# The modulation vectors of a two-layer trunk: the sum over 128 partitions by block transposes and row sums on VectorE and one product, with the result per partition

## The chip, the cores and the metric

The kernel runs on one core of a Trainium2 chip. The metric is the device time of one execution in microseconds. Before the change it is 1592.36 us, the median of three runs (1592.27 to 1593.94). A measurement of this kernel tells a difference of about 0.2% (3.2 us) from no change.

## The reference, cut to what matters

Two layers run over 256 latent tokens and 256 context tokens of width 1024. In each layer a conditioning vector `c` and a learned context vector `c_ctx` are turned into six modulation vectors of 1024 each; they scale and shift the tokens ahead of the mixer and ahead of the MLP, and gate what the two sub-layers add.

```python
def ada_mod(cond, w, b):
    return jnp.split(jax.nn.silu(cond) @ w + b, 6, axis=-1)
...
        sh1, sc1, g1, sh2, sc2, g2 = ada_mod(c[:, None, :], w_ada[l], b_ada[l])
        csh1, csc1, cg1, csh2, csc2, cg2 = ada_mod(c_ctx, w_ada[l], b_ada[l])
...
        u = x * (1.0 + sc1) + sh1
        p = split_proj(u @ w_in[l] + b_in[l])
...
        x = layer_norm(DEEPNORM_ALPHA * x + g1 * y, ln_g[l, 0], ln_b[l, 0])
        x = layer_norm(DEEPNORM_ALPHA * x + g2 * sq_relu_ffn(x * (1.0 + sc2) + sh2, w_ff1[l], w_ff2[l]),
                       ln_g[l, 1], ln_b[l, 1])
```

`w_ada[l]` is 1024 x 6144 in float32. The rest of a layer is a projection to 76 tiles of 128 channels, four branches (two convolutions, differential attention, neighbourhood attention), a merge by gates, an output projection and a squared-ReLU MLP of 4096.

## The kernel before

The large products are made on TensorE out of two parts of each float32 operand, a rounded one and what is left over: ScalarE writes the rounded part of a weight (`whi`), VectorE the rest (`wlo`), and three products are summed. The weights come in units of 128 x 1024 elements (512 KB) in one fixed order; each is loaded into a tile `raw`, split into `whi` and `wlo`, and used by 24 products or so. The tiles `raw`, `whi`, `wlo` and `araw` share ten buffers, at most three of each of the first three and two `araw` (`CAPS_W`). The step of this weight order that TensorE has reached is called the pace.

The order of all instructions on every engine is fixed ahead of the run by a planner. Each part of the work is a generator that yields one operation after another, with a priority (a smaller number goes first). The planner keeps a clock for each engine, gives each operation an assumed cost and puts next the operation that can start first, the one with the smaller number among equals. The engines then run their lists in that order, each instruction waiting for its own inputs. Where the planner sees TensorE without work for more than 0.8 us, it puts transposes of the identity in front (L272), whose results nobody reads. All loads and stores are issued by SP, in one list.

Priorities near the change: weight splits 3, merge of the branches 11, attention 10 to 16, the modulation of layer 0 12 and of layer 1 27 (`PRIO_ADA`), the long convolution's taps 90.

The modulation stands in `ada`. Group (0, 0), layer 0's first 2048 columns, has its own path at the start (`ada_first`) and isn't touched. The other five groups (l, g) of 2048 columns, (0, 1), (0, 2), (1, 0), (1, 1) and (1, 2), run one after another, (0, 1) from pace 44 (`ADA_PACE0`) and layer 1's from pace 108 in steps of 16. A group loads w_ada in 16 pieces `araw`, and VectorE, with ScalarE for some of the first ones, multiplies each row by the silu of the condition and sums over the eight blocks of 128 rows, into eight tiles `sums` of 128 x 512: four column blocks q by two conditions. Four of these tiles are borrowed from the four buffers `pad`, which the convolutions use too. What then is left is the sum over the 128 partitions:

- TensorE multiplies each `sums` with a matrix `ones` of 32 columns, one of which is 1: eight products with 512 columns, four column blocks side by side in the array, into `ada`.
- VectorE adds the bias (`ba`, loaded with b_ada repeated over 32 partitions) and writes `adrow`: the result along the free dimension, on a few partitions.
- TensorE transposes `adrow` in four blocks (`adT`), and VectorE copies 32 columns of it into `modT`: the result per partition, as the scaling of u needs it.
- For the gates (g > 0) four DMAs write rows of 2 KB from `adrow` to DRAM (`g`), from where they are later spread over the partitions as `row`.

The path that reads `modT` is `affine` and `to_u`; the path that reads `g` is `row_bcast`.

Of the kernel before, what the change touches and what calls it, by code (L numbers as in the profile page):

```python
# [9 lines left out]
F32 = mybir.dt.float32  # L10
# [25 lines left out]
ADA_PACE0 = 44  # L36
ADA_STEP = 16
ADA_SUMS = {(0, 1), (0, 2), (1, 0), (1, 1), (1, 2)}
# [283 lines left out]
class Kernel(Sched):  # L322
# [209 lines left out]
    def constants(self):  # L532
# [16 lines left out]
        self.ones = self.const([128, 2, 32], "ones")  # L549
        nc.vector.memset(self.ones.ap, 0.0)  # L550
        for c in range(2):
            nc.vector.memset(self.ones.ap[:, c, c:c + 1], 1.0)
# [11 lines left out]
        self.x2 = V(self.dp.tile([256, 1024], F32, name="x2"), (Buf(None),))  # L564

# [180 lines left out]
    def ada(self, l, g, pace):  # L746

        nc = self.nc
        yield self.wait("cs")
        yield self.wait("pace", pace)  # L750
        ba = yield self.s("", F32, "ba")
        yield self.dma(ba, self.rows4(self.b_ada[l, g * 2048:(g + 1) * 2048].rearrange("(q n) -> q n", q=4)), 1 << 18)
        sums = None
        if (l, g) in ADA_SUMS:
            sums = []
            pads = []
            for q in range(4):
                x = yield self.alloc("pad", name="sums")
                y = yield self.s("sums", F32, "sums")
                pads.append(x)  # L760
                sums.append((x[:, 0:512], y))
        ps = None
        for k in range(KD):
# [7 lines left out]
            if sums:  # L771
                for q in range(4):
                    w = raws[q // 2][:, (q % 2) * 512:(q % 2) * 512 + 512]
                    for c in range(2):
                        x, y = sums[q][c], self.cs[:, k, c:c + 1]
                        yield self.stt(x, w, y, x, ALU.mult, ALU.add) if k else self.affine_any(x, w, y)
                self.release(*raws)
                continue
            if ps is None:
                ps = yield self.alloc("ps", "ada", name="ada")  # L780
            yield self.mm([(ps.ap[32 * q:32 * q + 32, :], self.cs.ap[:, k, :],
                            raws[q // 2].ap[:, (q % 2) * 512:(q % 2) * 512 + 512], k == 0, k == KD - 1,
                            {"tile_position": (0, 32 * q)}) for q in range(4)], [ps], [*raws, self.cs], 1017)
            self.release(*raws)
        if sums:
            ps = yield self.alloc("ps", "ada", name="ada")
# [24 lines left out]
        self.release(row)  # L811

    @staticmethod
    def rows4(b):

# [1138 lines left out]
```

## Time and profile before

| what | value |
|---|---|
| median of three runs | 1592.36 us (1592.27 to 1593.94) |
| the profiled execution, its time | 1594.69 us |
| the profiled execution, its span from first to last instruction | 1592.9 us |
| mean granted TensorE clock | 0.998 |
| TensorE's products and weight loads | 8815 each |
| VectorE | 1308.8 us busy, 82% of the span |
| ScalarE | 876.2 us busy, 55% of the span |
| moved by DMA | 254.32 MB, 160 GB/s in the mean |

The busy time of PE (TensorE's products) is that of modelled ends; where rows of the timeline follow one another on PE, the distance of two starts says what a product takes of the engine, and its duration is the longer time until its result stands. DVE is VectorE, ACT ScalarE, POOL GpSimd, SP the engine that issues DMAs. VectorE's instructions overlap by some 0.1 us too where the next doesn't need the last one's result.

### The profile page before, as it was taken

How to read it: one execution, taken by the hardware profiler on the slowest of the kernel's cores; microseconds unless marked ns; L12 is line 12 of the kernel's file. 1: busy time of each engine (PE TensorE's matmuls, PEld its weight loads, DVE VectorE, ACT ScalarE, POOL GpSimd, SP SyncE). 2: the span in 40 equal slices, each digit the busy share in tenths (PEclk: the TensorE clock that was granted, in tenths of full speed). 3: DMA queues.
4: the chain of work that ended last, by engine and by line, in shares of the span. 5: the costliest groups of instructions: out<-in, count | busy, mean ns of one | idle time of the engine just before them, and what ended most of it. 6: DMA issues, size and time to landing. Idle time of an engine off the chain costs nothing. (4 is left out here: it accounts for less than half of the span.)

```text
span 1592.9 us, 23283 instructions
## 1 busy us (share of the span) xinstructions
PE 1571.9 (99%) x8815; PEld 1347.7 (85%) x8815; DVE 1308.8 (82%) x2210; ACT 876.2 (55%) x1413; POOL 12.2 (1%) x51
## 2 busy tenths in 40 slices
PE   9999999999999999999999999999999999999997
PEld 7778888887888888887887878989997999999997
DVE  4899999799998648896886795999999796785566
ACT  3576376456655544742423324766576786466553
POOL 0000000000000000000000000000000000000000
PEclk9999999999999999999999999999999999999999
DMA  9422222545553245455565644533443445645563
GB/s 357 145 69 79 99 74 80 184 173 169 169 179 126 81 159 197 152 198 179 177 206 177 213 160 156 188 126 132 147 139 120 146 159 171 240 146 186 198 224 108
DMA packets 80997, 254.32 MB, mean 160 GB/s; under 512 B 9060, under 2 KB 13924, under 8 KB 80884
## 3 DMA queue, kind: packets, MB, share of 16 engines
q1 hardware_dynamic: 80884, 252.83, 46.8%
q8 instruction: 69, 1.13, 0.3%
q14 instruction: 44, 0.36, 0.1%
HBM read 250.66 MB, written 2.13 MB: 159 GB/s over the span
## 5 line engine op out<-in xcount | busy, mean ns | idle before, releaser
L442 PE MATMUL mm<-u,whi 128*128 128x512 f32 (+1 forms) x3248 | 803.2, 340 | 1.8 <-ACT u L388 1.1
L442 PEld LDWEIGHTS mm<-u,whi 128*128 128x128 f32 x3248 | 557.7, 190 | 71.9 <-ACT u L388 4.2
L388 ACT ACTIVATE whi<-raw 128x1024 fp32r<-128x1024 f32 (+1 forms) x342 | 359.6, 1052 | 336.6 <-DVE wlo L395 127.3
L442 PE MATMUL mm<-u,wlo 128*128 128x512 f32 (+1 forms) x1624 | 542.6, 339 | 1.2 <-DVE wlo L395 0.8
L395 DVE TENSOR_TENSOR wlo<-raw,whi 128x1024 fp32r<-128x1024 f32 (+1 forms) x342 | 415.8, 1217 | 139.6 <-PE mm L442 65.2
L442 PEld LDWEIGHTS mm<-u,wlo 128*128 128x128 f32 x1624 | 306.4, 190 | 36.0 <-DVE wlo L395 1.8
L442 PE MATMUL f<-whi,a 128*128 128x512 f32 (+1 forms) x760 | 236.3, 388 | 0.0
L422 DVE SCALAR_TENSOR_TENSOR sums<-araw,cs,sums 128x512 f32<-128x512 f32 x280 | 194.8, 748 | 9.6 <-DMA araw<-in_w_ada 9.4
L442 PEld LDWEIGHTS f<-whi,a 128*128 128x128 f32 x760 | 142.3, 188 | 31.2 <-issue 2.5
L442 PE MATMUL f<-wlo,a 128*128 128x512 f32 (+1 forms) x380 | 147.1, 387 | 0.0
L422 DVE SCALAR_TENSOR_TENSOR conf<-glu,sm,conf 128x512 f32<-128x512 f32 (+1 forms) x240 | 138.9, 618 | 1.0
L442 PEld LDWEIGHTS f<-wlo,a 128*128 128x128 f32 x380 | 71.4, 188 | 14.2
L388 ACT ACTIVATE P<-S,st 128x512 f32<-128x512 f32 (+1 forms) x96 | 58.5, 613 | 25.1 <-DVE st L1229 24.9
L442 PE MATMUL wo<-whi,mg 128*128 128x512 f32 (+1 forms) x184 | 56.5, 382 | 0.0
L1229 DVE TENSOR_REDUCE st<-S 128x1 f32<-128x512 f32 (+1 forms) x96 | 55.2, 594 | 0.2
L442 PE MATMUL S<-qk 128*128 128x512 f32 (+1 forms) x192 | 49.9, 370 | 4.1 <-ACT qk L388 1.5
L388 ACT ACTIVATE qk<-ra 64x512 fp32r<-64x512 f32 (+1 forms) x71 | 40.3, 567 | 23.6 <-DVE ra L395 21.1
L388 ACT ACTIVATE gth<-mm,hb 128x512 f32<-128x512 f32 (+1 forms) x64 | 36.8, 575 | 29.6 <-PE mm L442 29.4
L388 ACT ACTIVATE a2f<-mm 128x512 f32<-128x512 f32 (+1 forms) x64 | 30.7, 481 | 31.7 <-PE mm L442 31.7
L395 DVE TENSOR_TENSOR a<-a2f,a 128x512 fp32r<-128x512 f32 (+1 forms) x64 | 35.4, 557 | 11.0 <-ACT a L388 10.6
L388 ACT ACTIVATE bh<-br,hb 128x512 f32<-128x512 f32 (+1 forms) x64 | 36.2, 571 | 13.8 <-PE br L442 13.5
L442 PEld LDWEIGHTS S<-qk 128*128 128x128 f32 x192 | 31.9, 189 | 13.8 <-ACT qk L388 4.0
(216 smaller groups left out, 1878.3 us busy)
## 6 DMA issues: line engine op xcount, KB each, us to landing
raw<-in_W SPq DMA_DIRECT2D x338, 512.0 KB
araw<-in_w_ada SPq DMA_DIRECT2D x80, 512.0 KB
a<-in_w_ada SPq DMA_DIRECT2D x32, 256.0 KB
bt<-in_rpb SPq DMA_DIRECT2D x32, 128.0 KB
raw<-in_W SPq DMA_DIRECT2D x8, 384.0 KB
row<-g SPq DMA_DIRECT2D x12, 256.0 KB
x<-in_x_t SPq DMA_DIRECT2D x8, 256.0 KB
row<-in_ln_g SPq DMA_DIRECT2D x8, 256.0 KB
```

Source lines behind the costliest of these rows:

```text
L388: lambda: nc.scalar.activation(out=out.ap, in_=in_.ap, func=func, **kw),
L395: return self._op(eng, cost, lambda: e.tensor_tensor(out=out.ap, in0=x.ap, in1=y.ap, op=op), [out], [x, y])
L422: return self._op("DVE", cost, lambda: nc.vector.scalar_tensor_tensor(out=out.ap, in0=x.ap, scalar=a(s), in1=y.ap, op0=op0, op1=op1), [out ...
L442: nc.tensor.matmul(out=out, lhsT=x, rhs=y, start=start, stop=stop, **kw)
L1229: yield self.dve(68 + 1.04 * nk, lambda: nc.vector.tensor_reduce(out=mx.ap, in_=S.ap, axis=AX.X, op=ALU.max, negate=True), [mx], [S])
```

## The change

The sum over the partitions is made in another way. For each of the eight tiles `sums` of a group, VectorE transposes its blocks of 32 x 32 elements in place of the block (4 x 16 blocks of a 128 x 512 tile, into `sumT`), and then sums each run of 32 along the free dimension. After this, a partition holds a sum over 32 of the 128 partitions for 16 columns, and eight such results of 16 columns fill 128 columns of `red`, the first 128 columns of the first `sums` tile. One product with a constant 128 x 128 matrix `four`, which has a 1 where two partitions agree modulo 32, adds the four quarters and leaves the sums on all partitions. Four small VectorE additions pick the quarter that belongs to each 32 partitions, add the bias, and write `modT`. The transposes and row sums run at priority 20 (`PRIO_SUM`).

With it the row `adrow`, its four TensorE transposes and `ba` go. The bias comes with the layer's small constants (`bada`, 48 columns more in SM). The gates are written to DRAM from `modT`: two DMAs for a group, each from 128 partitions x 8 elements, to 1024 single elements of 4 bytes in the order of the channels. `ones` goes, `four` is made at the start out of the identity by one reduction and one copy on VectorE. `ADA_PACE0` is 40 where it was 44, and all groups take this path (as all five did before).

```diff
-ADA_PACE0 = 44
+ADA_PACE0 = 40
 ADA_STEP = 16
-ADA_SUMS = {(0, 1), (0, 2), (1, 0), (1, 1), (1, 2)}
+PRIO_SUM = 20
...
-               ("dng", 1), ("bbr", 32), ("lng", 16), ("lnb", 16)):
+               ("dng", 1), ("bbr", 32), ("lng", 16), ("lnb", 16), ("bada", 48)):
...
+    def same_of_32(self):
+        nc = self.nc
+        t = self.const([128, 32], "four1")
+        src = self.ident.ap.rearrange("p (a i) -> p i a", a=4)
+        yield self.dve(200, lambda: nc.vector.tensor_reduce(out=t.ap, in_=src, axis=AX.X, op=ALU.add), [t], [self.ident])
+        o, x = self.four.ap.rearrange("p (a i) -> p a i", a=4), t.ap.unsqueeze(1).to_broadcast([128, 4, 32])
+        yield self.dve(200, lambda: nc.vector.tensor_copy(o, x), [self.four], [t])
+        self.signal("four")
...
-        if sums:
-            ps = yield self.alloc("ps", "ada", name="ada")
-            for h in range(2):
-                yield self.mm([(ps.ap[32 * q:32 * q + 32, :], self.ones.ap[:, c, :], sums[q][c].ap, c == 0, c == 1,
-                                {"tile_position": (0, 32 * q)}) for c in range(2) for q in (2 * h, 2 * h + 1)], [ps],
-                              [*sums[2 * h], *sums[2 * h + 1], self.ones], 1000)
-            for x, y in zip(pads, sums):
-                self.release(x, y[1])
-        row = yield self.s("", F32, "adrow")
-        yield self.tt(row, ps, ba, ALU.add)
-        self.release(ps, ba)
-        t = yield self.alloc("ps", "att", name="adT")
-        yield self.transposes([t[:, b * 128:b * 128 + 128] for b in range(4)],
-                              [row[:, b * 128:b * 128 + 128] for b in range(4)])
...
+        yield ("prio", PRIO_SUM)
+        red = pads[0][:, 0:128]
+        for q in range(4):
+            for c in range(2):
+                x = sums[q][c]
+                yield self.dve(600, lambda: nc.vector.transpose(out=t.ap, in_=x.ap), [t], [x])
+                o, z = red[:, 64 * c + 16 * q:64 * c + 16 * q + 16], t.re("p (b j) -> p b j", j=32)
+                yield self.dve(600, lambda: nc.vector.tensor_reduce(out=o.ap, in_=z.ap, axis=AX.X, op=ALU.add), [o], [z])
         self.release(t)
+        yield ("prio", PRIO_ADA if l else 12)
+        self.release(*pads[1:], *[y for x, y in sums])
+        ps = yield self.alloc("ps", "ada", name="ada")
+        yield self.mm([(ps.ap[:, 0:128], self.four.ap, red.ap[:, 0:128], True, True, {})], [ps], [red, self.four], 220)
+        bias = self.sm[l][:, _SM["bada"] + 16 * g:_SM["bada"] + 16 * g + 16]
+        for a in range(4):
+            p = slice(32 * a, 32 * a + 32)
+            o = self.modT[l][p, 16 * g:16 * g + 16, :]
+            src = ps.ap[p, 0:128].rearrange("p (s k a) -> p k s a", s=2, a=4)[:, :, :, a]
+            b = bias.ap[p].unsqueeze(2).to_broadcast([32, 16, 2])
+            yield self.dve(95, lambda: nc.vector.tensor_tensor(out=o.ap, in0=src, in1=b, op=ALU.add), [o], [ps, bias])
...
+            k0 = 16 * g + (0 if g == 1 else 8)
             for s in range(2):
-                for j in range(2):
-                    q = j + (0 if g == 1 else 2)
-                    yield self.dma(self.grow[l][g - 1][s][:, j * 512:(j + 1) * 512],
-                                   row[32 * q + s:32 * q + s + 1, :], 2048)
+                yield self.dma(self.grow[l][g - 1][s].re("o (k r) -> r (o k)", r=128), self.modT[l][:, k0:k0 + 8, s], 1 << 18)
```

How the lists of the engines stand now, at three places. On PE before, group (0, 2) ends like this (`mm` are projections out of u, `PT`, `S` and `o` attention, `br` the branches' products):

```order
L442 MATMUL mm<-u,wlo 128x512
L442 MATMUL ada<-sums,ones 32x512 x8
L503 MATMUL PT<-ident,P 128x128 x8
L442 MATMUL S<-qk 128x512 x2
L503 MATMUL adT<-ident,adrow 128x128 x4
L442 MATMUL mm<-u,whi 128x512 x2
```

In the changed kernel PE's list has for the same group:

```order
L442 MATMUL mm<-u,whi 128x512 x2
L442 MATMUL mm<-u,wlo 128x512
L442 MATMUL ada<-sums,four 128x128
L442 MATMUL br<-yd,whi 128x512 x2
L442 MATMUL br<-yd,wlo 128x512
```

Eight products and four transposes have become one product, and it stands among the products of the last branch, `br<-yd`, where the eight stood among attention.

On DVE before, the end of group (0, 2), its last multiplications, `adrow` and the copy into `modT` (`mod_90`), lies among weight splits and attention (`yd`, `pt`):

```order
L422 SCALAR_TENSOR_TENSOR sums<-araw,cs,sums 128x512 x4
L395 TENSOR_TENSOR wlo<-raw,whi 128x1024
L395 TENSOR_TENSOR yd<-olo,yd 64x512
L395 TENSOR_TENSOR adrow<-ada,ba 128x512
L395 TENSOR_TENSOR pt<-PT,pt 128x512 x2
L801 COPY mod_90<-adT 128x32
```

In the changed kernel DVE's list has the transposes and row sums of this group nearly in one run:

```order
L788 STREAM_TRANSPOSE sumT<-sums 128x512
L395 TENSOR_TENSOR wlo<-raw,whi 128x1024
L790 TENSOR_REDUCE sums<-sumT 128x16
L788 STREAM_TRANSPOSE sumT<-sums 128x512
L790 TENSOR_REDUCE sums<-sumT 128x16
L788 STREAM_TRANSPOSE sumT<-sums 128x512
L790 TENSOR_REDUCE sums<-sumT 128x16
```

Sixteen instructions have come in where one addition and one copy stood, with a weight split between them here and there; they depend on one another pair by pair through the one tile `sumT`.

At the third place, on PE before, in the end of the neighbourhood attention of layer 0, the planner had put transposes of the identity in three gaps (`o<-ident`, `PT<-ident`):

```order
L442 MATMUL o<-pt,v 128x256 x8
L272 MATMUL o<-ident 128x128 x7
L442 MATMUL o<-pt,v 128x256 x4
L503 MATMUL PT<-ident,P 128x128 x4
L272 MATMUL PT<-ident 128x128 x5
L503 MATMUL PT<-ident,P 128x128 x4
L442 MATMUL o<-pt,v 128x256 x8
L272 MATMUL o<-ident 128x128 x6
L442 MATMUL o<-pt,v 128x256 x4
```

In the changed kernel this end of the attention is spread between projections, and PE's list there is:

```order
```order
L503 MATMUL PT<-ident,P 128x128 x8
L442 MATMUL mm<-u,whi 128x512 x2
L442 MATMUL mm<-u,wlo 128x512
L442 MATMUL mm<-u,whi 128x512 x2
L442 MATMUL mm<-u,wlo 128x512
L442 MATMUL o<-pt,v 128x256 x12
L503 MATMUL PT<-ident,P 128x128 x4
```

The eighteen transposes of the identity are gone, and six projections of u stand between the attention's transposes and the products that read them.

More of the change, by code (lines that the diff above doesn't have):

```diff
@@ L548, in constants @@
         nc.gpsimd.memset(self.cs.ap, 0.0)
[L549 to L552, printed above, removed]
+        self.four = self.const([128, 128], "four")
         self.free.update(DVE=900.0, POOL=900.0, SP=SP_START)
@@ L750, in ada @@
         yield self.wait("pace", pace)
[L751 to L762, printed above, removed]
+        t = yield self.s("", F32, "sumT")
+        sums = []
+        pads = []
+        for q in range(4):
+            x = yield self.alloc("pad", name="sums")
+            y = yield self.s("sums", F32, "sums")
+            pads.append(x)
+            sums.append((x[:, 0:512], y))
         for k in range(KD):
@@ L770, in ada @@
                 raws.append(raw)
-            if sums:
[L772 to L779, printed above, removed]
-                ps = yield self.alloc("ps", "ada", name="ada")
@@ L781, in ada @@
-            yield self.mm([(ps.ap[32 * q:32 * q + 32, :], self.cs.ap[:, k, :],
-                            raws[q // 2].ap[:, (q % 2) * 512:(q % 2) * 512 + 512], k == 0, k == KD - 1,
-                            {"tile_position": (0, 32 * q)}) for q in range(4)], [ps], [*raws, self.cs], 1017)
-            self.release(*raws)
-        if sums:
-            ps = yield self.alloc("ps", "ada", name="ada")
-            for h in range(2):
-                yield self.mm([(ps.ap[32 * q:32 * q + 32, :], self.ones.ap[:, c, :], sums[q][c].ap, c == 0, c == 1,
-                                {"tile_position": (0, 32 * q)}) for c in range(2) for q in (2 * h, 2 * h + 1)], [ps],
-                              [*sums[2 * h], *sums[2 * h + 1], self.ones], 1000)
-            for x, y in zip(pads, sums):
-                self.release(x, y[1])
@@ L793, in ada @@
-        row = yield self.s("", F32, "adrow")
-        yield self.tt(row, ps, ba, ALU.add)
-        self.release(ps, ba)
-        t = yield self.alloc("ps", "att", name="adT")
-        yield self.transposes([t[:, b * 128:b * 128 + 128] for b in range(4)],
-                              [row[:, b * 128:b * 128 + 128] for b in range(4)])
-        out = self.modT[l][:, g * 16:(g + 1) * 16, :].re("p (q b) s -> p q b s", q=4)
-        src = t.ap.rearrange("p (b q r) -> p q b r", b=4, q=4)[:, :, :, 0:2]
@@ L801, in ada @@
-        yield self.dve(110, lambda: nc.vector.tensor_copy(out.ap, src), [out], [t])
-        self.release(t)
+            for q in range(4):
+                w = raws[q // 2][:, (q % 2) * 512:(q % 2) * 512 + 512]
+                for c in range(2):
+                    x, y = sums[q][c], self.cs[:, k, c:c + 1]
+                    yield self.stt(x, w, y, x, ALU.mult, ALU.add) if k else self.affine_any(x, w, y)
+            self.release(*raws)
+        yield self.wait("four")
+        yield ("prio", PRIO_SUM)
@@ new lines, in ada @@
+        red = pads[0][:, 0:128]
+        for q in range(4):
+            for c in range(2):
+                x = sums[q][c]
+                yield self.dve(600, lambda: nc.vector.transpose(out=t.ap, in_=x.ap), [t], [x])
+                o, z = red[:, 64 * c + 16 * q:64 * c + 16 * q + 16], t.re("p (b j) -> p b j", j=32)
+                yield self.dve(600, lambda: nc.vector.tensor_reduce(out=o.ap, in_=z.ap, axis=AX.X, op=ALU.add), [o], [z])
+        self.release(t)
+        yield ("prio", PRIO_ADA if l else 12)
@@ L810, in ada @@
             self.signal("grow", l, g - 1)
-        self.release(row)
-    @staticmethod
-    def rows4(b):
-        return b.unsqueeze(1).to_broadcast([4, 32, b.shape[1]])
     def ada_first(self, j, raws):
@@ L1838, in build @@
             self.spawn(self.silu_c(), 0)
+            self.spawn(self.same_of_32(), 60)
             self.spawn(self.ada_all(), 12)
@@ L1895, in _layout @@
         put("lnb", f["ln_b"][l].reshape(16, 128).T)
+        put("bada", f["b_ada"][l].reshape(48, 128).T)
     cT = np.stack([f["c"].reshape(8, 128), f["c_ctx"].reshape(8, 128)], -1).transpose(1, 0, 2).reshape(128, 16)
```

3 lines of the change are left out of this document (2 added, 1 removed).

## The prediction

> **What bounds the kernel now.** First the page's busy times, then TensorE's waits, then the busy time by stage.
>
> ```profile
> span 1592.9 us, 23283 instructions
> PE 1571.9 (99%) x8815; PEld 1347.7 (85%) x8815; DVE 1308.8 (82%) x2210; ACT 876.2 (55%) x1413; POOL 12.2 (1%) x51
> ```
>
> PE is busy for all but 21.0 us of the span. So an instruction taken off PE's list is worth its whole place there, as long as what PE does next is ready that much earlier. The question is whether VectorE, which gets the work instead, can still feed PE. The busy time by stage (busy us of PE, PEld, DVE and ACT, with counts) says where it has room:
>
> ```profile
> 360.00:380.00 20.00, 20.00 (x90) 16.21 (x89) 20.00 (x35) 13.91 (x20) 0.00 (x0) 1.00 0.55 183
> 380.00:400.00 20.00, 20.00 (x110) 15.50 (x109) 20.00 (x35) 12.46 (x21) 0.00 (x0) 1.00 0.48 158
> 400.00:420.00 20.00, 20.00 (x97) 16.77 (x96) 19.20 (x33) 13.35 (x24) 0.00 (x0) 1.00 0.58 187
> 420.00:440.00 20.00, 20.00 (x96) 16.73 (x96) 19.72 (x31) 12.10 (x22) 0.00 (x0) 1.00 0.42 143
> ...
> 500.00:520.00 20.00, 20.00 (x119) 17.54 (x118) 16.30 (x34) 14.44 (x30) 0.00 (x0) 1.00 0.25 82
> 520.00:540.00 20.00, 19.57 (x118) 16.06 (x118) 15.83 (x32) 13.17 (x28) 0.00 (x0) 1.00 0.15 51
> 540.00:560.00 20.00, 20.00 (x90) 16.56 (x89) 8.88 (x10) 9.03 (x12) 0.00 (x0) 1.00 0.44 144
> 1000.00:1020.00 20.00, 20.00 (x111) 17.09 (x110) 18.13 (x33) 14.21 (x23) 0.55 (x1) 1.00 0.44 156
> 1020.00:1040.00 20.00, 20.00 (x171) 20.00 (x170) 19.72 (x36) 17.04 (x31) 1.84 (x10) 1.00 0.73 239
> ```
>
> From 360 to 440 us, where the first group ends, VectorE has 1.1 us of 80 left (0 + 0 + 0.80 + 0.28), and yet PE never stops: what fills VectorE there is in part work that nobody needs soon. From 500 to 560 it has 19.0 us left (3.7 + 4.17 + 11.12). In layer 1's attention both are short at once, and PE stops:
>
> ```profile
> 1040.00:1080.00 40.00, 38.51 (x199) 31.96 (x199) 39.46 (x90) 25.12 (x48) 0.00 (x0) 1.00 0.32 112
> 1120.00:1160.00 40.00, 38.76 (x263) 35.45 (x262) 39.39 (x85) 25.31 (x44) 0.13 (x2) 1.00 0.40 138
> 1200.00:1240.00 40.00, 38.34 (x206) 31.90 (x205) 37.70 (x79) 25.76 (x51) 0.00 (x0) 1.00 0.32 104
> ```
>
> 1.49 + 1.24 + 1.66 = 4.4 us of PE are lost in these three stretches.
>
> **What is taken off PE.** The products with `ones` by stage, one window for each group (the first and the last of five, and the sum), and then the timeline of PE around the first group's four transposes:
>
> ```profile
> 380.00:400.00 20.00, 2.47 (x16) 1.00 0.48 158
> ...
> 940.00:950.00 10.00, 1.94 (x16) 1.00 0.32 110
> sum 80.00, PE 12.52; mean PE 2.50
> ...
> 394.66 0.60 PE L503 MATMUL adT<-ident,adrow 128*128 128x128 f32 x4
> 395.02 0.71 PE L442 MATMUL mm<-u,whi 128*128 128x512 f32 x2
> ```
>
> 12.5 us for the products, in which almost nothing lies beside them, since PE's next product starts as they end. The four transposes hold PE from 394.66 to 395.02, 0.36 us; five groups make 1.8. Removed: 12.5 + 1.8 = 14.3 us.
>
> **What is put on PE.** One float32 product of 128 columns for each group. The nearest row is a constant float32 product of 256 columns:
>
> ```profile
> L442 PE MATMUL ms<-osq,on 128*128 128x256 f32 x8 | 2.4, 377 | 0.0
> ```
>
> That is 0.30 us for a record. The lists have 40 products with `ones` and the trace 80 records, so a float32 product makes two records, 0.60 us for 256 columns and 0.30 for 128. Bounds: 0.09 us, as one of the four transposes above (0.36 / 4), and 0.60, that row without the halving. I take 0.30, the row it is nearest to: 1.5 us for five.
>
> **Transposes of the identity.** The planner filled three gaps of the neighbourhood attention with them, and PE ran them:
>
> ```profile
> 529.19 0.93 PE L272 MATMUL o<-ident 128*128 128x128 f32 x7
> 529.87 1.08 PE L442 MATMUL o<-pt,v 128*128 128x256 f32 x4
> ...
> 531.22 0.71 PE L272 MATMUL PT<-ident 128*128 128x128 f32 x5
> 531.98 0.81 PE L503 MATMUL PT<-ident,P 128*128 128x128 f32 x4
> ...
> 533.90 0.81 PE L272 MATMUL o<-ident 128*128 128x128 f32 x6
> 534.47 0.74 PE L442 MATMUL o<-pt,v 128*128 128x256 f32 x2
> ```
>
> From their starts to the next product's: 0.68 + 0.76 + 0.57 = 2.0 us. In the new order projections of u stand in these gaps and the fillers are gone. So 2.0 us go if those projections were due anyway, and nothing if the wait turns up elsewhere. I count 2.0.
>
> **What VectorE gets.** Block transposes don't occur before. The nearest rows are the lane shuffle, which also moves elements between partitions, its neighbour of the same size, a row sum of 512, and the weight split of 1024 for a slower case:
>
> ```profile
> L1147 DVE STREAM_SHUFFLE rsh<-ra 128x256 f32<-128x256 f32 x16 | 7.1, 444 | 0.1
> L395 DVE TENSOR_TENSOR ra<-ra,rsh 128x256 f32<-128x256 f32 x16 | 6.7, 422 | 0.3
> L395 DVE TENSOR_TENSOR wlo<-raw,whi 128x1024 fp32r<-128x1024 f32 x334 | 408.1, 1223 | 139.1 <-PE mm L442 65.2 <-PE f L442 30.0 <-ACT whi L388 23.2
> L1229 DVE TENSOR_REDUCE st<-S 128x1 f32<-128x512 f32 x64 | 42.8, 683 | 0.1
> ...
> 981.03 0.69 DVE L395 TENSOR_TENSOR yf<-f,row 128x512 f32<-128x512 f32 x1 [0.30 <-PE f L442]
> 981.76 0.69 DVE L395 TENSOR_TENSOR yacc<-yf,yacc 128x512 f32<-128x512 f32 x1
> 982.37 1.22 DVE L395 TENSOR_TENSOR wlo<-raw,whi 128x1024 fp32r<-128x1024 f32 x1
> ```
>
> The shuffle takes as long as plain arithmetic (444 against 422 ns). So I take 0.69 us for a transpose of 512, as for arithmetic of 512. In the timeline an instruction that needs the one before starts 0.73 us after it (981.03 to 981.76), another 0.61 us (981.76 to 982.37). A pair of transpose and dependent row sum takes 0.73 + 0.61 = 1.34 us; eight pairs 10.7 us a group. The four additions at the end are worth about what `adrow` and its copy were:
>
> ```profile
> L395 DVE TENSOR_TENSOR adrow<-ada,ba x5: 672/691/699, 391.6 to 944.3; 128x512 f32<-128x512 f32 x5
> L801 DVE COPY mod<-adT x5: 182/187/198, 395.6 to 947.3; 128x32 f32<-128x32 f32 x5
> ```
>
> 0.69 + 0.19 = 0.88 us go, and four additions of 32 columns, at the copy's 0.19 each, cost 0.75. Net 10.7 us a group, 53 us in all. VectorE would be busy for about 1362 of 1580 us, 86%. Bounds for a transpose: 0.44 us (the shuffle's, were 512 as cheap as 256) and 1.22 us (the split of 1024, were each element to count twice).
>
> [...]
>
> **What hides these 53 us.** The new rows have priority 20. Weight splits (3), merge (11) and attention (10 to 16) go first, the convolution taps (90) and layer 1's multiplications (27) come later, so the group's own end and the next group are what is late. Counted by the products ahead of each in PE's list, at 0.227 us for 512 columns,
>
> ```profile
> 1433.54 21.79 PE f L442 x96
> ```
>
> (21.79 / 96), the five products stand 47, 54, 16, 35 and 79 us of products later than the first `ones` product of each group did. Layer 0's last group thus ends near 540 us, and its reader is `affine`; layer 1's last ends near 1015, and its reader is much later:
>
> ```profile
> L402 DVE TENSOR_SCALAR t<-mod x3: 168/168/169, 599.8 to 1373.1; 128x16 f32<-128x16 f32 x3
> ```
>
> 599.8 and 1373.1: nobody waits for `modT`. If the cover fails, a row that PE waits for comes behind a 0.7 us row of the new kind, up to 16 times a group. From 1000 to 1040 us, where the last group ends, VectorE has only 2.15 us left (1.87 + 0.28), so its taps move into the attention that already costs PE 4.4 us. I allow nearly half of that, 2.0 us, for new waits; bounds 0 and 21.4 (two groups, 10.7 each, in full stretches).
>
> **DMA and the rest.** The five loads `ba` and sixteen stores `g` go, eight stores of 1024 elements come, behind which SP's next weight loads queue. The loads' own row:
>
> ```profile
> q1 hardware_dynamic: 80884, 252.83, 46.8%
> ```
>
> 0.468 x 16 x 1592.9 us / 80884 = 147 ns for a packet of 3.1 KB in the mean. By bytes, 4 bytes cost nothing; at the mean packet's time, 64 packets on each of 16 engines take 9.4 us, 18.9 for a group's two stores. Packets of 4 bytes are nearer to nothing, and I count 0. The store itself is read only by `row`, long after it. The constants at the start grow by 128 x 48 x 4 bytes, 25 KB, a twentieth of one weight unit, and `four` is made while VectorE waits for the condition anyway:
>
> ```profile
> 2.62 0.17 DVE L402 TENSOR_SCALAR cth<-cth 128x16 f32<-128x16 f32 x1 [1.25 <-ACT cth L388]
> ```
>
> A start four weights earlier moves the first group's loads forward by 4 x 24 x 0.227 = 22 us, into a stretch without PE waits: 0.
>
> **The sum.** -14.3 + 1.5 - 2.0 + 2.0 = -12.8 us. The profiled span of 1592.9 becomes 1580.1; around it lie 1.8 us (its time is 1594.69), so that execution would take 1581.9. The runs' median is 2.3 us (0.15%) below that execution; from 1592.36 I get **1579.6 us**. With all waits absent and the bound of 0.09 us for the product it is 1592.36 - 14.3 + 0.5 - 2.0 = 1576.6.
>
> **Rivals.**
>
> - VectorE becomes the bound where it is full. For it: 1.1 us left from 360 to 440, 2.15 from 1000 to 1040. Against it: 19.0 us left from 500 to 560, and the low priority. If half the rows of the first and last group stand ahead of a row PE waits for, 10.7 us come back instead of the 0 from layer 0 and 2.0 from layer 1 counted: 1592.36 - 14.8 + 10.7 = 1588.3, between 1585 and 1592.
> - The stores of single elements hold up weight loads. Three loaded weights lie ahead of PE's use, each 24 x 0.227 = 5.4 us, 16.3 in all. At 18.9 us a group 2.6 us go through to PE, with the first transfer behind it some 3: four groups give 10 to 12 us, 1590 to 1592. Against it: a 4-byte packet at the price of a 3.1 KB one. [...]
> - Slower: a block transpose takes 1.22 us, not 0.69. The product `ada` stands in PE's list where the planner thinks 0.6 us for each, so PE waits at it: 0.54 x 8 = 4.3 us a group, 21.6 in five, 1579.6 + 21.6 = 1601. It turns the sign from 12.8 / 40 = 0.32 us more for each, above about 1.0 us. For it: no transpose in this trace; against it: the shuffle's row.
>
> **How the numbers follow.** The forecast gets 0.64, VectorE as the bound 0.16, the stores 0.07, the slow transpose 0.13. The bound of 0.2%, about what a measurement of this kernel can tell from no change, lies at 1589.2 and 1595.5. Of VectorE's 0.16, 0.09 fall under 1589.2, the rest on no change; the stores are no change; of the slow transpose 0.11 is slower and 0.02, with part of the wait hidden, no change. Faster 0.73, same 0.16, slower 0.11. The range reaches from 1576 (all waits absent) to 1595, which takes in the first two rivals with their bounds and leaves the slow transpose out.
>
> **What would show it.** In the changed profile: PE's records fall by 80 + 20 + 18 - 10 = 108; `ada<-sums,four` takes about 0.3 us a group; L788 and L790 take about 0.7 us each, some 53 us between them; nothing waits for `mod`; `wlo` rows still end ahead of their products. Wrong would be: waits of PE at `ada` of more than 1 us a group (slow transposes or full VectorE), waits of ScalarE's `whi` for DMA behind the stores (the second rival), or more than 2 us of new waits from 1040 to 1240.

## The result, and the profile after

| kernel | median | runs | ratio to before, 95% interval |
|---|---|---|---|
| before | 1592.45 us (1592.27 to 1593.94) | 4 | |
| changed | 1613.11 us (1612.14 to 1613.54) | 4 | 1.0129 [1.0117, 1.0141] |

The change makes the kernel 20.7 us slower; the forecast was 12.8 us faster. The changed kernel's profiled execution took 1612.14 us, with a span of 1610.3 and a mean granted clock of 0.991. Its busy times, from the page:

```profile
span 1610.3 us, 23122 instructions
PE 1563.9 (97%) x8707; PEld 1345.7 (84%) x8707; DVE 1360.9 (85%) x2304; ACT 874.1 (54%) x1408; POOL 11.9 (1%) x51
```

PE lost 108 records and VectorE got 52.1 us, both much as forecast. PE's busy time fell by only 8.0 us, where 14.8 were forecast; products at half clock, shown below, put some 7.3 us back. And PE is now idle for 46.4 us (1610.3 - 1563.9), where it was 21.0. The busy time by stage (columns as before: the stretch, its length, then PE, PEld, DVE, ACT and POOL, then granted clock) says where. The changed kernel:

```profile
440.00:480.00 40.00, 30.71 (x145) 25.48 (x144) 29.60 (x63) 20.96 (x42) 0.00 (x0) 0.87 0.51 122
520.00:560.00 40.00, 33.08 (x154) 27.15 (x153) 38.29 (x57) 14.53 (x21) 0.00 (x0) 0.91 0.39 131
880.00:920.00 40.00, 36.45 (x160) 29.55 (x159) 20.45 (x32) 13.02 (x18) 0.00 (x0) 1.00 0.68 180
1040.00:1080.00 40.00, 35.84 (x213) 30.40 (x212) 34.22 (x72) 21.92 (x39) 0.00 (x0) 0.95 0.56 164
```

The kernel before, in the same stretches:

```profile
440.00:480.00 40.00, 40.00 (x188) 33.41 (x188) 39.78 (x68) 23.55 (x41) 0.00 (x0) 1.00 0.56 191
520.00:560.00 40.00, 39.57 (x206) 32.62 (x206) 24.70 (x42) 22.20 (x39) 0.00 (x0) 1.00 0.30 97
880.00:920.00 40.00, 40.00 (x178) 33.10 (x178) 31.31 (x43) 12.34 (x16) 0.00 (x0) 1.00 0.68 220
1040.00:1080.00 40.00, 38.51 (x199) 31.96 (x199) 39.46 (x90) 25.12 (x48) 0.00 (x0) 1.00 0.32 112
```

Four holes of 9.3, 6.5, 3.6 and 2.7 us, 22.0 in all, and in three of them the granted clock falls too (0.87, 0.91 and 0.95). A busy PE at half clock counts as busy, so what this costs is not seen in the holes. Most of the rest of the new idle time lies between 960 and 1040 us. In the first, third and fourth hole VectorE, too, does less than before; in the second it does far more (38.29 against 24.70 us). They are two different things. PE's waits (engine and line, what it waited for, us in total, times, longest) name them:

```profile
PE PT L503 <- DVE P L402: 9.3, 1, 9.3
PE f L442 <- DVE wlo L395: 5.4, 4, 2.5
PE br L442 <- DVE yd L395: 3.5, 1, 3.5
PE S L442 <- DVE qk L402: 3.5, 5, 1.9
PE br L442 <- ACT yd L388: 3.1, 1, 3.1
```

**The first hole** is a DMA's. SP's own queue around it (start, us, what was issued):

```profile
441.40 1.01 SPq L433 DMA_DIRECT2D g<-mod  x2
442.50 0.53 SPq L433 DMA_DIRECT2D araw<-in_w_ada  x1
443.12 0.39 SPq L433 DMA_DIRECT2D raw<-in_W  x1
443.56 0.42 SPq L433 DMA_DIRECT2D bt<-in_rpb  x1
```

The two stores of group (0, 1)'s gates, 2048 single elements, are followed by three loads. The third is a small table, `bt`, of attention's biases. In VectorE's timeline its reader, and the four `sums` multiplications behind that, stand still:

```profile
449.78 0.16 DVE L1271 RECIPROCAL st<-st 128x1 f32<-128x1 f32 x1
458.42 0.43 DVE L395 TENSOR_TENSOR S<-S,bt 128x256 f32<-128x256 f32 x1 [8.48 <-DMA bt<-in_rpb]
458.76 1.67 DVE L402 TENSOR_SCALAR sums<-araw,cs 128x512 f32<-128x512 f32 x4
```

The load was issued at 443.56 and landed at 458.4, after 14.8 us, as `bt`'s own row says; its median is 3.6:

```profile
DMA to landing us min/median/max: 2.9/3.6/14.8
```

PE's wait of 9.3 us for `P` is this wait passed on: no row of `P` can be made until VectorE's list moves. The holes in the stretches from 880 and from 1040 us come behind layer 1's two pairs of stores; the last store is issued at 1036.3 us. Group (0, 2)'s pair, issued at 569 us, costs nothing: PE is busy for all of the 40 us from 560.

**The second hole** stands at the end of attention, where PE waits twice for `yd`. VectorE's timeline there:

```profile
541.77 2.73 DVE L422 SCALAR_TENSOR_TENSOR sums<-araw,cs,sums 128x512 f32<-128x512 f32 x4
544.53 0.69 DVE L395 TENSOR_TENSOR olo<-o,olo 64x512 f32<-64x512 f32 x1
545.25 2.74 DVE L422 SCALAR_TENSOR_TENSOR sums<-araw,cs,sums 128x512 f32<-128x512 f32 x4
547.91 1.22 DVE L395 TENSOR_TENSOR wlo<-raw,whi 128x1024 fp32r<-128x1024 f32 x1
549.16 0.69 DVE L395 TENSOR_TENSOR yd<-olo,yd 64x512 fp32r<-64x512 f32 x1
```

and PE's (in brackets the wait and what ended it):

```profile
545.93 0.50 PE L442 MATMUL br<-yd,whi 128*128 128x512 f32 x1 [3.15 <-ACT yd L388]
549.90 0.79 PE L442 MATMUL br<-yd,whi 128*128 128x512 f32 x1 [3.47 <-DVE yd L395]
```

What PE needs, `olo` and then `yd`, stands behind eight multiplications of group (0, 2), 5.5 us, whose result nobody needs for another 60 us.

**The clock** falls to a half in the first, second and fourth hole. Four narrow stretches of the changed kernel, first the first wait and what follows it, then what follows the second and the fourth hole:

```profile
456.90:466.40 9.50, 0.24 (x2) 0.00 (x0) 7.81 (x18) 5.28 (x9) 0.00 (x0) 0.73 0.50 167
466.40:471.40 5.00, 4.97 (x13) 4.01 (x14) 5.00 (x8) 2.40 (x5) 0.00 (x0) 0.50 0.38 113
549.90:553.30 3.40, 3.40 (x8) 2.72 (x9) 3.26 (x5) 1.63 (x2) 0.00 (x0) 0.50 0.23 93
1075.80:1082.60 6.80, 6.22 (x15) 4.88 (x16) 6.67 (x15) 3.67 (x8) 0.00 (x0) 0.51 0.01 2
```

After its wait of 9.3 us PE runs 5.0 us at clock 0.50. Products of 512 columns start 0.43 us apart there (469.69 to 470.12), and 0.23 us apart behind it (471.94 to 472.17), so about half of the stretch is lost, 2.5 us; the other two, counted in the same way, cost 1.7 and 3.1 us. These 7.3 us are counted as busy. While PE waits, a lower clock costs nothing: in the first stretch it is already down to 0.73. The length of the wait doesn't decide alone. The third hole, with 2.5 us as its longest wait, has a clock of 1.00; the fourth, with 1.9 us as its longest, has the most half clock.

### The profile page after: what moved, and what is told of

Read it like the earlier page. It is cut to its first block, busy times and chain, and to the rows that moved or that the text cites. A ratio compares the mean times of both kernels' runs of the same rounds, so it can differ in the third digit from the quotient of the medians.

```text
span 1610.3 us, 23122 instructions
## 1 busy us (share of the span) xinstructions
PE 1563.9 (97%) x8707; PEld 1345.7 (84%) x8707; DVE 1360.9 (85%) x2304; ACT 874.1 (54%) x1408; POOL 11.9 (1%) x51
## 5 line engine op out<-in xcount | busy, mean ns | idle before, releaser
L442 PE MATMUL mm<-u,whi 128*128 128x512 f32 (+1 forms) x3248 | 804.8, 341 | 2.3 <-ACT u L388 1.3
L442 PEld LDWEIGHTS mm<-u,whi 128*128 128x128 f32 x3248 | 557.3, 190 | 72.8 <-ACT u L388 4.6
L442 PE MATMUL mm<-u,wlo 128*128 128x512 f32 (+1 forms) x1624 | 542.5, 339 | 1.1 <-DVE wlo L395 1.1
L388 ACT ACTIVATE whi<-raw 128x1024 fp32r<-128x1024 f32 (+1 forms) x342 | 359.8, 1053 | 329.5 <-DVE wlo L395 99.9
L395 DVE TENSOR_TENSOR wlo<-raw,whi 128x1024 fp32r<-128x1024 f32 (+1 forms) x342 | 414.4, 1213 | 116.4 <-PE mm L442 44.0
L442 PEld LDWEIGHTS mm<-u,wlo 128*128 128x128 f32 x1624 | 306.1, 190 | 36.1 <-DVE wlo L395 1.9
L442 PE MATMUL f<-whi,a 128*128 128x512 f32 (+1 forms) x760 | 234.6, 387 | 0.0
L422 DVE SCALAR_TENSOR_TENSOR sums<-araw,cs,sums 128x512 f32<-128x512 f32 x280 | 196.0, 746 | 15.9 <-DMA araw<-in_w_ada 15.7
L442 PEld LDWEIGHTS f<-whi,a 128*128 128x128 f32 x760 | 142.3, 188 | 28.8
L442 PE MATMUL f<-wlo,a 128*128 128x512 f32 (+1 forms) x380 | 147.5, 388 | 5.4 <-DVE wlo L395 5.4
L422 DVE SCALAR_TENSOR_TENSOR conf<-glu,sm,conf 128x512 f32<-128x512 f32 (+1 forms) x240 | 137.6, 613 | 1.0
L442 PEld LDWEIGHTS f<-wlo,a 128*128 128x128 f32 x380 | 71.4, 188 | 21.3 <-DVE wlo L395 7.1
L388 ACT ACTIVATE P<-S,st 128x512 f32<-128x512 f32 (+1 forms) x96 | 58.7, 615 | 35.9 <-DVE st L1222 35.7
L442 PE MATMUL S<-qk 128*128 128x512 f32 (+1 forms) x192 | 50.0, 379 | 6.9 <-DVE qk L402 3.5
L442 PE MATMUL wo<-whi,mg 128*128 128x512 f32 (+1 forms) x184 | 56.5, 382 | 0.0
L388 ACT ACTIVATE qk<-ra 64x512 fp32r<-64x512 f32 (+1 forms) x67 | 37.8, 565 | 24.1 <-DVE ra L395 22.8
L388 ACT ACTIVATE gth<-mm,hb 128x512 f32<-128x512 f32 (+1 forms) x64 | 36.8, 575 | 21.4 <-PE mm L442 21.1
L442 PEld LDWEIGHTS S<-qk 128*128 128x128 f32 x192 | 33.1, 195 | 17.6 <-DVE qk L402 4.8
L388 ACT ACTIVATE bh<-br,hb 128x512 f32<-128x512 f32 (+1 forms) x64 | 36.3, 573 | 20.7 <-PE br L442 20.4
L503 PE MATMUL PT<-ident,P 128*128 128x128 f32 x240 | 36.1, 275 | 10.8 <-DVE P L402 9.3
L388 ACT ACTIVATE a2f<-mm 128x512 f32<-128x512 f32 (+1 forms) x64 | 30.7, 482 | 26.3 <-PE mm L442 26.3
```

Of the source, the lines that this page charges most:

```text
L388: lambda: nc.scalar.activation(out=out.ap, in_=in_.ap, func=func, **kw),
L395: return self._op(eng, cost, lambda: e.tensor_tensor(out=out.ap, in0=x.ap, in1=y.ap, op=op), [out], [x, y])
L422: return self._op("DVE", cost, lambda: nc.vector.scalar_tensor_tensor(out=out.ap, in0=x.ap, scalar=a(s), in1=y.ap, op0=op0, op1=op1), [out ...
L442: nc.tensor.matmul(out=out, lhsT=x, rhs=y, start=start, stop=stop, **kw)
L503: nc.tensor.transpose(o.ap, i.ap, ident.ap)
```

## The experiments

Two theories stood at the start for the 33.5 us between forecast and result: the **stores** of single elements hold up the loads behind them, and the **order** (or the load) of VectorE's list makes PE wait near 530 us. The kernel before was timed again beside each experiment, at 1591.8 to 1592.2 us in the median.

**e1: the stores in runs of 32 bytes.** The changed kernel with `modT` laid out so that a partition's eight values lie together, and stored so; the gates come out in a permuted order. No other instruction differs.

```diff
-        self.modT = [self.const([128, 48, 2], f"mod{l}") for l in range(DEPTH)]
+        self.modT = [self.const([128, 2, 48], f"mod{l}").re("p s k -> p k s") for l in range(DEPTH)]
...
-                yield self.dma(self.grow[l][g - 1][s].re("o (k r) -> r (o k)", r=128), ...
+                yield self.dma(self.grow[l][g - 1][s].re("o (r k) -> r (o k)", r=128), ...
```

> The changed kernel with the same lists of instructions, but modT is laid out so that a store of a gate is 128 runs of 8 contiguous elements (32 bytes) on both sides, where it was 1024 single elements. The gates stand in DRAM in another order of the channels, so the residual sums use permuted gates. Theory S (the stores of single elements hold up the loads behind them): PE's 9.3 us wait for P at 457 us and the 8.5 us wait of S for bt go, landing of a store falls from 10.7 us to about 3, and the time falls by the three gaps and the clock behind them to 1578 to 1590 us. Rival V (VectorE's 52 us of new work make PE wait, whatever the stores are): 1608 to 1614 us.

Measured: 1590.82 us, 0.9989 [0.998, 0.9999]. The stores' row of the page's DMA issues (KB each, median us to landing):

```profile
g<-mod SPq DMA_DIRECT2D x8, 4.0 KB, 1.5
```

against the changed kernel's

```profile
g<-mod SPq DMA_DIRECT2D x8, 4.0 KB, 10.7
```

The same bytes, from the same partitions, in an eighth of the packets (the 88512 of the queue become 81344, 7168 fewer): 22.3 us of the kernel's time go (1613.11 - 1590.82), and with them the wait for `bt`. PE's holes behind layer 1's stores go too: it is busy for 40.00 us from 880 to 920 and for 37.92 from 1040 to 1080 (before 38.51). Two thirds of the 33.5 us are the stores. 11.2 us are left.

**e2: the same stores in the kernel before.** Its 16 stores of 2 KB rows are made from `modT`, 512 single elements each; all else is the kernel before but for a few rows of the lists, so the sums are too.

```diff
-                    yield self.dma(self.grow[l][g - 1][s][:, j * 512:(j + 1) * 512],
-                                   row[32 * q + s:32 * q + s + 1, :], 2048)
+                    k0 = 16 * g + (0 if g == 1 else 8) + 4 * j
+                    yield self.dma(self.grow[l][g - 1][s][:, j * 512:(j + 1) * 512].re("o (k r) -> r (o k)", r=128),
+                                   self.modT[l][:, k0:k0 + 4, s], 2048)
```

> The kernel before with one edit: its sixteen stores of a gate's half are made from modT as 512 single elements each, as in the changed kernel, and nothing else is changed (the order of the lists stays the same but for a few rows). Theory S: slower than before by 5 to 20 us, with waits of loads of about 10 us behind each of the four pairs of stores. Rival V: no change, 1590 to 1595 us.

Measured: 1624.93 us, 1.0202 [1.0186, 1.0217], 32.7 us more than before, and more than the 5 to 20 that were expected. PE's waits in it:

```profile
PE PT L503 <- ACT P L388: 13.7, 2, 13.2
PE mm L442 <- DVE wlo L395: 10.8, 4, 5.3
```

`bt` lands after 19.5 us at the longest, and VectorE waits 16.9 us for it. So the stores do it in the old order of the lists as well as in the new, and for weight splits (`wlo`) as well as for attention (`P`).

**e3: rows of 512 bytes.** The changed kernel, with one transpose on PE that brings 128 x 16 of `modT` to 16 rows of 128, a copy out of PSUM, and stores of eight rows each.

```diff
+            t = yield self.alloc("ps", "att", name="gT")
+            yield self.transposes([t[0:16, 0:128]], [self.modT[l][:, k0:k0 + 8, :].re("p k s -> p (k s)")])
+            rows = yield self.s("", F32, "grows")
+            yield self.copy_any(rows[0:16, 0:128], t[0:16, 0:128])
...
-                yield self.dma(self.grow[l][g - 1][s].re("o (k r) -> r (o k)", r=128), self.modT[l][:, k0:k0 + 8, s], 1 << 18)
+                yield self.dma(self.grow[l][g - 1][s].re("o (k r) -> (o k) r", r=128), rows[s:16:2, 0:128], 4096)
```

> The changed kernel, with the gates transposed on TensorE before they are stored: one transpose of 128 x 16, one copy out of PSUM, and two stores of 8 rows of 512 bytes for a group. It computes what the reference asks for. Theory S: PE gets 4 x 0.1 us more work and no stalls behind the stores: 1578 to 1588 us, faster than before. Rival V: 1606 to 1614 us.

Measured: 1592.46 us, 1.0 [0.999, 1.0009]. The stores are cured, and the kernel is back at the time before, not at the forecast. What is left is above all one wait of 7.6 us, here not at `br` but at the `o` ahead of it. In VectorE's timeline of e3:

```profile
530.06 4.72 DVE L422 SCALAR_TENSOR_TENSOR sums<-araw,cs,sums 128x512 f32<-128x512 f32 x7
534.69 1.22 DVE L395 TENSOR_TENSOR wlo<-raw,whi 128x1024 fp32r<-128x1024 f32 x1
535.83 0.68 DVE L395 TENSOR_TENSOR olo<-o,olo 64x512 f32<-64x512 f32 x1
536.43 1.27 DVE L395 TENSOR_TENSOR pt<-PT,pt 128x512 fp32r<-128x512 f32 x2
```

and in PE's:

```profile
537.16 1.86 PE L442 MATMUL o<-pt,v 128*128 128x256 f32 x7 [7.57 <-DVE pt L395]
```

Seven multiplications of group (0, 2) stand ahead of `pt`.

**e4: the element stores from ScalarE's queue.** The changed kernel, its stores issued by ScalarE and not by SP.

```diff
-                yield self.dma(self.grow[l][g - 1][s].re("o (k r) -> r (o k)", r=128), self.modT[l][:, k0:k0 + 8, s], 1 << 18)
+                yield self._op("ACT", 60, lambda: nc.scalar.dma_start(out=o.ap, in_=x.ap), [o], [x], lag=DMA_LAG, table=None)
```

> The changed kernel with the eight stores of single elements issued by ScalarE into its own DMA queue instead of SP's. Theory S, if it is the order within SP's queue that holds up the loads: the loads pass the stores, 1578 to 1592 us. Theory S, if the stores hold up the DMA engines or the memory for all queues: 1600 to 1616 us, with landings of loads of over 10 us behind them. Rival V: 1606 to 1614 us.

Measured: 1613.75 us, 1.0134 [1.0118, 1.0149], as without it. The stores land 16.5 us after their issue (median), and PE's wait for `P` is 10.5 us where it was 9.3:

```profile
PE PT L503 <- DVE P L402: 10.5, 1, 10.5
```

The stores' 8320 packets (1040 for each) stand in a queue of their own here (q10 of the page, the loads in q1), and yet `bt` lands after 16.7 us at the longest and the time is 0.6 us from the changed kernel's. So it isn't SP's list in which the loads queue, but something that both queues share; what that is, this run doesn't show.

**e5: the earlier start alone.** The kernel before with `ADA_PACE0 = 40`.

```diff
-ADA_PACE0 = 44
+ADA_PACE0 = 40
```

> The kernel before with ADA_PACE0 = 40 and nothing else. Theory L (what is left once the stores are mended, some 11 us, is the block transposes of layer 0's groups, which push the second group's multiplications into the end of the attention near 530 us, where VectorE has no room): the earlier start alone ends the second group earlier, takes the fillers' gaps near 530 us away, and gives 1585 to 1590 us. Rival P (the earlier start itself brings the multiplications into the wrong stretch): 1594 to 1600 us, with waits of PE near 530 us.

Measured: 1589.24 us, 0.9987 [0.9979, 0.9996]: 2.8 us less by the medians, 0.6 to 3.3 by the interval, with 8797 records on PE, 18 fewer. These are the 18 transposes of the identity: the three small gaps of the attention go by the earlier start, not by the new sum.

**e6 and e7: one layer alone.** Rows of 512 bytes and pace 40 in both; e6 makes the new sum in layer 1's three groups only, e7 in layer 0's two only.

```diff
+NEW = {(1, 0), (1, 1), (1, 2)}
...
+        if (l, g) not in NEW:
+            yield from self.ada_end(l, g, sums, pads, ba)
+            return
```

> Layer 1's three groups end in the new way, with the gates stored as in e3_rows (one TensorE transpose, rows of 512 bytes); layer 0's two groups end as in the kernel before; ADA_PACE0 = 40. Theory L: no wait near 530 us, 1578 to 1584 us, faster than before and than e3_rows by about 10 us. Rival W (the new work costs PE waits wherever it runs, in layer 1 too): 1588 to 1594 us.

> The opposite part alone: layer 0's two groups end in the new way, with the gates stored as in e3_rows; layer 1's three as in the kernel before; ADA_PACE0 = 40. Theory L: the wait near 530 us of 7 us stays, with a stretch of lower clock behind it, 1594 to 1600 us, slower than before. Rival W: between before and e3_rows, 1590 to 1594 us.

Measured: e6 1584.55 us, 0.9952 [0.9939, 0.9964], just above the 1578 to 1584 expected; e7 1596.45 us, 1.0026 [1.0016, 1.0037]. Against e5, layer 1's groups win 4.7 us and layer 0's lose 7.2. So the second hole belongs to layer 0, and e7 has it to the same 7.6 us as e3. By the prediction's terms three groups would win 3 x (14.3 - 1.5) / 5 = 7.7 us; 2.5 of the 3.0 that are missing stand in e6's waits, at the last group's product, which waits for the last row sum (done at 1012.4 us, the product starts at 1012.5; the view names the small row `st` behind it), and at a weight split of the MLP with a transpose and a row sum a few rows ahead of it in VectorE's list:

```profile
PE ada L443 <- DVE st L403: 1.5, 1, 1.5
...
PE f L443 <- DVE wlo L396: 1.0, 1, 1.0
```

**e8: VectorE's work taken out, the order kept.** e1's kernel with the same lists, but layer 0's 32 transposes and row sums not issued, so that layer 0's modulation is left out from there on.

```diff
-                yield self.dve(600, lambda: nc.vector.transpose(out=t.ap, in_=x.ap), [t], [x])
+                yield self.dve(600, lambda: l and nc.vector.transpose(out=t.ap, in_=x.ap), [t], [x])
```

> e1_runs32 with the same lists, out of which the 32 block transposes and row sums of layer 0's two groups are left out, so that layer 0's second and third group of modulation vectors are not those of the reference (and the gates stay permuted). Theory L: with 10.7 us less on VectorE ahead of it, the wait of PE at br for yd near 535 us falls from 7 us to under 2 and the lower clock behind it goes, 1578 to 1583 us. Rival O (the order of the lists alone makes the wait, whatever VectorE's load is): the wait stays, 1587 to 1591 us.

Measured: 1588.77 us, 0.9978 [0.9969, 0.9987], 2.0 us less than e1. The hole is there as before, although VectorE now has a third of the stretch free:

```profile
520.00:560.00 40.00, 32.78 (x142) 26.56 (x142) 26.33 (x38) 14.50 (x20) 0.00 (x0) 0.91 0.35 118
```

e1 has 32.77 there, with VectorE at 37.93. So the added rows are not what makes PE wait. What is left of the theory is the order: what stands ahead of what in VectorE's list.

**e9: one number, the order alone.** e3's kernel (its one transpose written as a plain PE operation), and the multiplications of group (0, 2) at priority 17, behind attention's 10 to 16, where they ran at 12.

```diff
+        if (l, g) == (0, 2):
+            yield ("prio", 17)
```

> The kernel with stores as rows of 512 bytes (1592.46), and one number changed: the multiplications of group (0, 2) run at priority 17 where they ran at 12, so that they stand behind the last attention (15 and 16) in VectorE's list. No instruction is added or removed, VectorE has the same work. Theory O (the order of the list makes the wait of 7.95 us at 529 us): the wait goes, and with it the 10.2 us of half clock behind it (5.1 us of products): 1592.5 - 7.7 - 5.1 = about 1580, and nobody waits for the group that ends later. Rival L (VectorE has too much work up to 540 us, 10.7 us a group more): the same work still has to be done there, the wait turns up at another reader within the next 30 us, at most 1 to 3 us are won: 1589 to 1592.

Measured: 1580.47 us, 0.9931 [0.9917, 0.9946], 12.0 us less than e3 and 11.3 less than the kernel before, timed beside it at 1591.81. Its page and its stage:

```profile
span 1580.1 us, 23143 instructions
PE 1554.5 (98%) x8711; PEld 1340.2 (85%) x8711; DVE 1360.5 (86%) x2308; ACT 872.8 (55%) x1408; POOL 11.9 (1%) x51
```

```profile
520.00:560.00 40.00, 40.00 (x178) 33.10 (x178) 35.51 (x49) 14.39 (x19) 0.00 (x0) 1.00 0.69 224
```

VectorE's busy time is that of the changed kernel (1360.9), PE has no hole, and no half clock behind it. This is within a microsecond of the forecast time, and better than both kernels. Of the 5.1 us that were expected from e3's half clock, its timeline shows 1.9.

**e10: layer 1's sums later.** e9 with layer 1's transposes and row sums at priority 27.

```diff
-        yield ("prio", PRIO_SUM)
+        yield ("prio", 27 if l else PRIO_SUM)
```

> As e9, and layer 1's transposes and row sums at priority 27, as its multiplications, where they stood at 20 like layer 0's. Theory O carried on (what waits is what stands behind these rows in the list): the waits of 1.4 us at f<-wlo near 970 us and of 1.5 us at the last group's product near 1012 us get shorter, 1 to 2.5 us less than e9: about 1578. Rival: layer 1's waits are VectorE's load, and the time is that of e9 within 0.5 us or more than it.

Measured: 1580.88 us, 0.9932 [0.9918, 0.9947], e9's time. PE's wait at `ada` has gone, and another has come, at the transposes of the MLP's result:

```profile
PE uT L503 <- ACT yacc L388: 1.1, 1, 1.1
```

Layer 1's 2.5 us can't be had by this number; whether it is load or another place in the list stays open.

**e11: the order alone in the changed kernel.** The changed kernel, stores and all, with e9's two lines.

> The changed kernel itself, stores of single elements and all, with the one number of e9: group (0, 2)'s multiplications at priority 17. If the two causes are separate and add, the stores keep their 22.3 us and the time is e9's plus 22: 1613.1 - 12.8 = about 1600. Rival: part of the 22 us was the second store's stall falling together with the wait near 540 us, so that the two together cost less than the sum when one goes: 1603 to 1608.

Measured: 1605.75 us, 1.0089 [1.0072, 1.0106], 7.4 us less than the changed kernel and 25.3 more than e9. By the medians the stores cost 3.0 us more here than in e1 (25.3 against 22.3), by the profiled spans 1.2 us (1603.3 - 1580.1 against 1610.3 - 1588.3), so how far the two causes add stays open. The time lies in the rival's range, but the rival's reason isn't seen: group (0, 2)'s pair of stores costs nothing in either kernel (PE busy for 40.00 us from 560 to 600). In e11 the hole in the stretch from 520 has gone, and the stretch from 880 to 920 has a clock of 0.96 where the changed kernel had 1.00. What sets this was not tried.

**e12: the elements far apart.** e9 and, beside its rows, the changed kernel's stores into a scratch in DRAM that nobody reads, each element at the start of 512 bytes of its own.

```diff
+        self.scr = [V(self.dp.tile([1024, 128], F32, name=f"scr{s}"), (Buf(None),)) for s in range(2)]
...
+            for s in range(2):
+                yield self.dma(self.scr[s].re("(k r) e -> r k e", r=128)[:, :, 0], self.modT[l][:, k0:k0 + 8, s], 1 << 18)
```

> The kernel of e9 (1580.5: row stores, group (0, 2)'s multiplications at 17), and beside its row stores two more stores for each group of gates: the same 1024 single elements from modT, into a scratch of 1024 x 128 in DRAM that nobody reads, each element to the start of a row of 512 bytes of its own. Packets in number and size are those of the changed kernel's stores (e11, whose lists are these otherwise: 1605.75). Theory A (elements of 4 bytes that lie beside one another in DRAM are written one after the other, and that holds up the rest): far apart they cost little, 1580 to 1586, and no wait for bt of several us near 450 us. Theory N (it is the number of packets, wherever they go): the stall stays, 8 to 10 us of landing and the wait for bt, 1600 to 1610.

Measured: 1583.73 us, 0.9944 [0.9927, 0.9961]. As many packets of the same size (88640 on the queue against e9's 80320) cost 3.3 us more than e9, not 25.3. The landing of these stores, and then of `bt`:

```profile
DMA to landing us min/median/max: 2.9/3.8/4.6
```

```profile
DMA to landing us min/median/max: 3.6/3.7/3.8
```

So the price isn't that of the number of packets: it goes with elements which are neighbours in DRAM. Near ones cost 22.0 us more here than far ones (1605.75 against 1583.73). Why neighbours do is not shown: e12 also spreads a store's elements over 512 KB in place of 4 KB, so that the distance of two elements and the size of the stretch of DRAM aren't told apart.

## Why the prediction was wrong

**What is taken off PE: right, but that e9 meets the sum is luck.** The records fell by 108, as counted. In e9, which has the change without its two faults, PE is busy for 17.4 us less than before (forecast 14.3 - 1.5 + 2.0 = 14.8) and idle for 4.6 us more (forecast 2.0): 12.8 us of span, the forecast's sum, because two misses of 2.6 us cancel. (By the medians it is 11.3 us.) 1.5 us of the first miss are half clock behind a wait of 1.1 us at 657 us in the kernel before, which e9 doesn't have. By parts, the earlier start gives 2.8 us (e5), layer 1's groups 4.7 (e6) and layer 0's 4.1 (e9 against e6), where 2.0, 7.7 and 5.1 were forecast, and 2.0 to be lost again in waits. The new product was put at 0.30 us for a group. In the changed kernel's PE timeline it takes 0.14, from its start to the next product's:

```profile
438.83 0.39 PE L442 MATMUL ada<-sums,four 128*128 128x128 f32 x2
438.97 0.71 PE L442 MATMUL mm<-u,whi 128*128 128x512 f32 x2
```

**What VectorE gets: right.** The changed kernel's rows of the new tile:

```profile
L788 DVE STREAM_TRANSPOSE sumT<-sums x40: 686/711/712, 394.3 to 1032.1; 128x512 f32<-128x512 f32 x40
L790 DVE TENSOR_REDUCE sums<-sumT x40: 670/686/689, 402.3 to 1032.8; 128x16 f32<-128x512 f32 x40
```

0.71 and 0.69 us where 0.69 was taken, and 52.1 us in all where 53 were. The third rival, 1.22 us for a transpose, falls. The lane shuffle was the right row to go by.

**The stores at nothing: wrong, 22.3 us.** The prediction said "Packets of 4 bytes are nearer to nothing, and I count 0". Its upper bound, 9.4 us for a store, was close to the 10.7 measured. The row it was taken from, a mean packet, says nothing of neighbouring elements, so the bound was near by chance; but the bound was there, and was worth more than 0.07. The rival that used it went wrong in the next step, "Three loaded weights lie ahead of PE's use". That holds for weights. The first load behind the stores that someone waited for was `bt`, which is loaded shortly before its use, and which had VectorE's whole list behind it. So a hole of 9.3 us came at the first pair, and not 2.6.

**"So the group's own end and the next group are what is late": wrong, 10 to 12 us.** That is e1 and e3 against e9; with the stores of single elements it is 7.4 (e11). This was read from the priorities, and the first half is right: (0, 1)'s rows at 20 end late. But the next group, (0, 2), which begins when (0, 1) is done, is late only until it may start. Its first multiplications on VectorE, before the change:

```profile
403.08 1.27 DVE L402 TENSOR_SCALAR sums<-araw,cs 128x512 f32<-128x512 f32 x3
```

In the changed kernel the last row sum of (0, 1) comes first:

```profile
437.66 0.68 DVE L790 TENSOR_REDUCE sums<-sumT 128x16 f32<-128x512 f32 x1
```

and then the row at 458.76 that is shown above; in e3 and e9, without the stores' hole, it is 450 to 451 us. From then on these multiplications run at 12, ahead of attention at 15 and 16, and begun some 47 us later they meet the attention's last rows, on which PE depends. e8 shows that the rows at 20 are not themselves in the way, e9 that this place in the list is. The bound of 21.4 us for new waits was wide enough, but it was priced as VectorE being full; it had the right size for the wrong reason.

**The fillers: 2.0 against 2.8, for another reason.** They go by `ADA_PACE0` alone (e5). The prediction counted the earlier start at 0 and took the fillers' absence from the list as the absence of the gap. In the changed kernel the fillers are gone, and two waits of 6.6 us together stand 10 us further on: that no filler stands in a list doesn't mean that no wait does.

**Nobody waits for `modT`: right.** But for the stores, layer 0's groups have no reader before `affine` at 613.4, and none of the holes is there.

**Left out: the clock.** Products at half clock cost the changed kernel some 7.3 us. For the second hole e9 against e3 gives 12.0 us; from 520 to 560 us e3 has 8.7 us of idle PE and 3.8 us of products at half clock, 1.9 us lost, and e9 neither. No term and no rival had it.

**The second rival** (stores) had the right cause and too small a price, 10 to 12 us; **the first** (VectorE the bound) named the right engine, but the wrong place: it looked from 360 to 440 and from 1000 to 1040 us, and took the 19.0 us left from 500 to 560, where the second hole came, as a point against itself. And e8 and e9 show that VectorE isn't a bound there. The two causes, with the clock behind them, make 33.5 us, which takes the time over the upper end.

## What to carry to other kernels

A store whose elements of 4 bytes are neighbours in DRAM was not priced by its bytes or its packets here (it landed in 10.7 us, the same packets far apart in 3.8): turn it first, so that runs of 32 bytes (landed in 1.5 us, e1) or rows of 512 (`bt` lands after 5.7 us at the longest, e3) go out, and look which load behind it is wanted soonest, not which is the largest. When work is moved to a later priority, look at what it releases: work that starts later at an unchanged high priority can land in front of the very rows that bound the kernel. Read a new list for what stands ahead of the rows that the critical engine waits for, since an engine with a third of its time free can still be late (VectorE in e8, 26.33 us busy of 40).

## What the runs showed of the hardware

- 2048 neighbouring elements of 4 bytes held up loads of other tiles for some 10 us: in the changed kernel `bt` landed after 14.8 us where its median is 3.6, and after 16.7 us with the stores issued from ScalarE's queue (e4). A store of 1024 such elements landed in 10.7 us; as 32-byte runs it landed in 1.5 us (e1), with its elements far apart in 3.8 us (e12).
- The granted clock fell to 0.50 in three of the changed kernel's four holes, and the products made at that clock cost 2.5, 1.7 and 3.1 us on top of the waits. It fell behind short waits too: the longest in the fourth hole is 1.9 us, and in the kernel before a wait of 1.1 us ends at 657 us, ahead of 3.4 us at 0.50. In the third hole, with a wait of 2.5 us, it stayed at 1.00. What sets it is not shown.
- VectorE's transpose of 32 x 32 blocks was about as fast as plain arithmetic on float32: 0.711 us for 128 x 512 in the changed kernel, where an addition of that size took 0.69.
